# Four column strips of a modulation product in one tile, and the second layer's later ones moved into the dense feed-forward

## The chip, the cores and the metric

One core of a Trainium2 chip runs the kernel. The time is device microseconds from start to end of one launch. Three runs of the kernel before took 2573.72, 2575.47 and 2582.24 us; their median is 2575.47 us.

## What is computed

Two layers of a backbone work on 256 latent tokens behind 256 context tokens, with 1024 features each. A layer is a modulated norm, a token mixer of three parts (S5, gated DeltaNet, Mamba-2) and a residual, then a second modulated norm, a feed-forward and a residual. The first layer has a dense feed-forward, the second one a top-2-of-8 expert feed-forward. Cut to what matters here:

```python
for i in range(DEPTH):                                   # DEPTH = 2
    ml = jnp.split((sc @ ada_w[i] + ada_b[i])[:, None, :], 6, axis=-1)   # latent modulation
    mc = jnp.split(sx @ ada_w[i] + ada_b[i], 6, axis=-1)                 # context modulation
    h_lat = modulate(x_lat, norm1_g[i], ml[0], ml[1])
    h_ctx = modulate(x_ctx, norm1_g[i], mc[0], mc[1])
    y_ctx, y_lat = token_mixer(h_ctx, h_lat, w_in[i], s5_p, gdn_p, m2_p, not last)
    x_lat = x_lat + ml[2] * (y_lat @ w_out[i])
    x_lat = x_lat + ml[5] * ffn(modulate(x_lat, norm2_g[i], ml[3], ml[4]))
    # the same for x_ctx in the first layer
```

`ada_w[i]` has 1024 rows and 6144 columns, float32, 24 MB a layer. It meets only two vectors, `sc` and `sx`, so its product is a reading of 24 MB with little arithmetic.

## The kernel before

The work of the two layers is traced by one class, `Net`, and put in order by a scheduler. `band(b)` sets a priority: instructions traced in a lower band stand earlier, as far as their inputs and their buffers let them. All loads go through one queue, SP's, in that order, and each engine executes its instructions in that order. Pools of buffers are stacked on a left and a right side of the on-chip memory. A pool that is opened where another one lay waits for what used that place.

**The modulation product.** `ada` (L176) works out a third `g` of a layer's 6144 columns: 2048 columns, taken as four strips of 512. For each of the eight tiles `k` of 128 rows, and each strip, it loads a tile of `ada_w` (L184) and issues one matmul with the 32 columns of `sc` as the stationary operand (L157, through `mm`). The four strips use four different groups of 32 columns of the PE array (`tile_position`) and four groups of 32 partitions of one PSUM bank. The finished bank is copied to `adasb` (L190), transposed in four pieces (L193) and added to `mods` (L198). Third 0 of layer 0 is worked out in another function, `first_inputs`. Thirds 1 and 2 of both layers are traced in `mixer`, with tiles of one strip (`wd=512`, 256 KB, two buffers); third 0 of layer 1 is traced behind `mixer(0)` in the main function, with tiles of two strips (512 KB, four buffers). Third 1 holds the factor of the mixer's residual and the shift of the second norm, third 2 that norm's scale and the factor of the feed-forward's residual.

**The mixer.** `mixer` (L1206) projects the normed input, then runs three parts whose instructions are interleaved: gated DeltaNet (`gdn`, tiles `gd_` and `iv_`, a recurrence over chunks of 128 tokens), Mamba-2 (`m2`, tiles `m_`), and the read-out of S5 (`s5_out`, L621). `s5_out` takes four quarters in turn. A quarter loads `s5U`, `s5X`, eight pieces of `s5D` (L638) and two `s5V` (L643), all but `s5V` with one buffer, and issues 24 matmuls (48 records) on them. After each two quarters the result goes through a transpose, a skip and a gelu to memory (`geD`, L672). `s5_gate` (L677) then reads it back (`s5gL`, `s5gH`, L685), multiplies it with `s5_w_glu` and writes `yD` (L697). The other two parts write `yD` too (L1021 and L1189). At the end the pool `yo` is opened, on the same side as the S5 read-out and over its place; `yD` is read back and split in two parts (L1379, L1380), and `out_proj` (L1389) multiplies it with `w_out` and adds the residual (L1407).

Layer 0 has the pool `ad` of the modulation tiles on the left, below `s5_out`'s pool `s5o`; the right side has the pool of `gdn`, whose lowest tiles are `gd_ncs`, `gd_oss`, `gd_rs` and `iv_X`.

**Feed-forwards.** `ffn` (L1410) takes the 22 tiles of hidden features in four strips of 6, 5, 6 and 5: gate and up products, silu, and the down product added to the residual. `moe` (L1450) loads all experts' weights (`mwr`, L1651), whose first loads wait for residuals of the second mixer.

Of the kernel before, what the change touches and what calls it, by code (L numbers as in the profile page):

```python
# [10 lines left out]
F32 = mybir.dt.float32  # L11
# [4 lines left out]
PSUM = bass.MemoryType.PSUM  # L16
# [3 lines left out]
KT = 8  # L20
T = 512
# [10 lines left out]
# Places of the layers' parts in the schedule (bands relative to the layer's own), buffers and PSUM banks.  # L32
# [53 lines left out]
class Net:  # L86
# [41 lines left out]
    @contextmanager  # L128
    def band(self, b):
        """Instructions traced inside are scheduled behind those of lower bands."""  # L130
        tc, outer = self.tc, self.cur
        if b == outer:
            yield
            return
        self.cur, old = b, tc.cur_priority
        tc.cur_priority = self.bands.get(b, int(b * 100000))
        yield
        self.bands[b] = tc.cur_priority
        self.cur, tc.cur_priority = outer, old
# [9 lines left out]
    def psum_split(self, **banks):  # L149
        """The PSUM banks of each use from here on in the trace."""  # L150
        self.turn = {tag: cycle(ids) for tag, ids in banks.items()}
# [24 lines left out]
    def ada(self, l, g, p, tag, bufs, wd=1024):  # L176
        nc = self.nc
        W = self.A["ada_w"][l]
        ps = self.ps("ad")
        for k in range(KT):  # L180
            w = []
            for c0 in range(g * 2048, (g + 1) * 2048, wd):
                t = p.tile([128, wd], F32, name="ada", tag=tag, bufs=bufs)
                nc.sync.dma_start(t, W[k * 128:(k + 1) * 128, c0:c0 + wd])  # L184
                w += [t[:, i:i + 512] for i in range(0, wd, 512)]
            for j in range(4):
                self.mm(ps[32 * j:32 * j + 32, :], self.sc[:, k, :], w[j],
                        start=(k == 0), stop=(k == KT - 1), tile_position=(0, 32 * j))
        sb = p.tile([128, wd], F32, name="adasb", tag=tag, bufs=bufs)[:, :512]
# [10 lines left out]
    def mod_ab(self, l, which, ks=slice(0, KT)):  # L200
        """Per-feature factor and shift of one modulated norm, [128, 8, 2]; the factors of the tiles ks are worked out."""
# [10 lines left out]
    def first_inputs(self, p, pw, hH, hL):  # L212
        """Shift and scale of the first norm, two feature tiles at a time, their part of the normed input, and its products with
        the first columns of w_in as they come."""
# [41 lines left out]
    def rsqrt(self, pool, out, v, shape, s=1.0, e=EPS, eps_ap=None, bufs=1):  # L256
        nc = self.nc
        y0 = pool.tile(shape, F32, name="rs_y", tag="rs_y", bufs=bufs)
        h = pool.tile(shape, F32, name="rs_h", tag="rs_h", bufs=bufs)
        t = pool.tile(shape, F32, name="rs_t", tag="rs_t", bufs=bufs)  # L260
# [7 lines left out]
    def norm_stats(self, pool, x, early):  # L268
        """1 / rms of x: [128, 8, n], the same in all partitions; early: the band of the sums of squares."""
# [14 lines left out]
    def norm_tile(self, pool, x, r, ab, hH, hL, k, perm=False):  # L284
        """Feature tile k of the norm times a plus b; x: [128, 8, T]."""
# [20 lines left out]
    def wload(self, src, nk, ncol, keep=None):  # L306
        """src: [nk*128, ncol] in DRAM; the parts of each k tile, in the pool keep if there is one."""
# [18 lines left out]
    def mm3(self, ps, w, h, first, last, tiles=None):  # L326
        """ps += w^T h over the k tiles, w and h as (high, low) lists per tile."""
# [7 lines left out]
    def proj(self, l, c0, ncol, h, t0):  # L335
        """[ncol <= 128 columns of w_in]^T h -> PSUM [ncol, T - t0]."""
# [10 lines left out]
    def exp_acc(self, p, out, x, shape):  # L347
# [17 lines left out]
        # below the range of the reduction the result is zero  # L365
        nc.vector.scalar_tensor_tensor(out, x, -87.0, y, op0=OP.is_ge, op1=OP.mult)

# [1 line left out]
    def s5_tables(self, l, side, lo, hi, U=None, B=None, lam=None):  # L369
        """Per-layer tables of the S5 scan in chunks of 8 tokens, kept in DRAM; lo and hi are the bands of its Vector part and  # L370
        of the rest. With U, the first table is applied to it at once and the powers go to lam."""
# [8 lines left out]
        with tc.tile_pool(name="s5tab", bufs=1, side=side, reuse_waits="tile") as p, self.band(lo):  # L380
# [27 lines left out]
            # gamma = (lam_bar - 1) / lam  # L408
# [25 lines left out]
            # the powers 8, 16, ... 256 for the scan  # L434
# [15 lines left out]
            # the powers act on B, and their conjugates on conj(C)  # L450
# [15 lines left out]
            for q in range(4):  # L466
# [17 lines left out]
                with self.band(hi):  # L484
# [26 lines left out]
                    # k-th lag: rows (direction, input); lag 0 sums the directions  # L511
# [30 lines left out]
    def s5_inputs(self, p, j, u, U):  # L542
        """Channel tile j of the scan's input in chunks: U[(token in chunk, channel), group, chunk]."""
# [17 lines left out]
    def s5_own(self, G, U, B, g0):  # L561
        """The chunks' own states of four groups, to the places of the states that enter the next chunks."""
# [11 lines left out]
    def s5_states(self, l, U, B, side):  # L574
        """The chunks' own states by the table in DRAM."""
# [9 lines left out]
    def s5_scan(self, l, p, B, lam):  # L585
        """The states that enter the chunks, kept in DRAM: a scan by doubled strides, up and down."""
# [3 lines left out]
        def add(e, i0, n):  # L590
            """B[i] += lam^(8 * 2^e) B[i - 2^e], n places i0, i0 + 2 * 2^e, ..."""
# [29 lines left out]
    def s5_out(self, l, uD, UD, XD, yD, t0, side):  # L621
        """Scan outputs, skip, gelu and gate; the result goes to yD[0:4]."""
# [78 lines left out]
    def smalls(self, l, p, tp, h):  # L701
# [15 lines left out]
        # softplus = max(x, 0) + log1p(exp(-|x|)), log1p by 2 atanh(e / (2 + e))  # L717
# [15 lines left out]
        # both parts, four heads of each in turn  # L733
# [10 lines left out]
        # cs: decay from the chunk's start through each token; de: from each token to the end; tot  # L744
# [16 lines left out]
    def decay_quad(self, p, sm, t, h0, out, tag, bufs):  # L761
        """out[s, h, c] = decay between tokens s and c of chunk t (forward above the diagonal)."""
# [13 lines left out]
    def conv_silu(self, p, ps, w, b, out):  # L776
        """ps: [128, n] of whole 256-token segments; out: [128, n]."""
# [18 lines left out]
    def gdn_tok(self, p, tp, src, n, out, ss, t_first, h):  # L796
        """Token-major copy of one head's [128, n] tile to DRAM, and each token's sum of squares."""
# [32 lines left out]
    def gdn_prep(self, p, tp, kT, qT, bs, sm, t0):  # L830
        """Decayed key products of the chunks and the inverses of their 16 x 16 diagonal blocks."""
# [55 lines left out]
    def gdn(self, l, p, kT, qT, vD, kD, prep, nrm, bs, ks, qss, sm, szD, yD, t0, b0):  # L887
        """kT: [128, 4, 512]; qT: [128, 4, 512 - t0]; vD, kD: token-major [128, chunk, head, 128]; b0: the first band of
        the layer."""
# [21 lines left out]
        def inverses(gr):  # L911
            """(I + U)^-1 of strictly triangular matrices, by doubling the diagonal blocks; U[s] = beta[s] kw[s]."""
# [32 lines left out]
        def step(t, d, Y, last):  # L945
            """One chunk of the recurrence."""
# [52 lines left out]
        def outs(pair):  # L999
            """rmsnorm and gate; the query norm and its scale act only through eps"""  # L1000
# [51 lines left out]
    def m2_decays(self, p, sm, WD, first):  # L1052
        """WD[s, chunk, head, c]: the weight of token s's step in token c, before the product of their B and C."""
# [13 lines left out]
    def m2(self, l, p, g, sm, mD, WD, yD, t0):  # L1067
        """One group of 8 heads, a generator of three stages for each pair of chunks. mD: x (4 tiles), silu(z) (4), B, C, feature-major; the normed and gated result goes
        to yD."""
# [17 lines left out]
        def states(pair):  # L1087
            """The inputs of two chunks and the states entering them."""
# [81 lines left out]
        def gate(pair, ins):  # L1170
            """Gate and norm of the outputs of two chunks."""
# [11 lines left out]
            r = p.tile([128, 256], F32, name="m2_r", bufs=1)  # L1183
            self.rsqrt(p, r, pn[:, :256], [128, 256], 1.0 / 512)
# [21 lines left out]
    def mixer(self, l):  # L1206
# [35 lines left out]
        if l == 1:  # L1242
            pa, qa = self.pool("ad", sa)
# [24 lines left out]
        with self.band(b0 + q_["sc"]):  # L1268
            # as large as the input's pool at least, so the next pool keeps clear of it
            pt, qt = self.pool("s5t", sb)  # L1270
            XD = self.s5_scan(l, pt, B, lam)
# [57 lines left out]
        # the second gates, and the inputs of the state space part, one kind first or in turn  # L1329
# [14 lines left out]
        for g in (1, 2):  # L1344
            with self.band(b0 + q_[f"ab{g}"]):
                self.ada(l, g, pa, "ad", 2, 512)
        with self.band(b0 + q_["sb"]):
            self.s5_out(l, uD, UD, XD, yD, t0, sa)
        with self.band(b0 + q_["m2"]):
            p, q2 = self.pool("m2", sb)  # L1350
            # the first stage of a pair of chunks is traced before the last one of the pair before it
# [31 lines left out]
        qa.close()  # L1383
        if l == 0:
            qg.close()
            qm.close()
        self.dbg(f"x_mix{l}", self.xT)

    def out_proj(self, l, part, y, t0):  # L1389
        """The rows of w_out in the blocks part of 512."""  # L1390
# [7 lines left out]
    def residual(self, l, mod0, m, ps, t0, perm=False):  # L1398
        """x[m] += gate * ps"""
# [10 lines left out]
    def ffn(self, l, side):  # L1410
# [10 lines left out]
        for nj in (6, 5, 6, 5):  # L1421
# [22 lines left out]
            j0 += nj  # L1444
        q.close()
# [4 lines left out]
    def moe(self, l):  # L1450
# [13 lines left out]
        # units of the first weights, where later tokens and results go  # L1464
# [34 lines left out]
    def route(self, p, rw, ab, htp, Pm, gate, rk, iota, cnt):  # L1499
        """Top-2 routing and the dispatch of the tokens. The tokens are normed without the factors a and shifts b of their  # L1500
        features here; the logits take them by the router's rows, the experts' inputs after the dispatch."""
# [367 lines left out]
    def run(self):  # L1869
# [9 lines left out]
        with self.band(R["ff"]):  # L1879
            self.ffn(0, "right")  # L1880
# [72 lines left out]
```

## Time and profile before

| | before |
|---|---|
| runs | 2573.72, 2575.47, 2582.24 us |
| profiled execution: span, mean granted clock | 2572.8 us, 0.968 |
| PE busy | 2380.3 us, 93% |
| VectorE (DVE) busy | 1866.4 us, 73% |
| ScalarE (ACT) busy | 1441.9 us, 56% |
| GpSimd (POOL) busy | 375.1 us, 15% |
| moved by DMA | 543.87 MB, mean 211 GB/s |

The profile has no other time of its own execution than its span; the median of the runs is 2.7 us above that. Stages by the first and last instructions of their tiles: the first mixer runs to about 760 us, the dense feed-forward to about 1165, the second mixer to about 1735, the experts to the end. A line number of a matmul says little, since nearly all are recorded at L157; they are told apart by the tiles that they write and read (`bank<-ada,sc` is the modulation product). [...] "PEclk" and the clock column of a window are the granted TensorE clock as a share of full speed (2.4 GHz). DMA is the mean busy share of the 16 DMA engines.

### The profile page before, as it was taken

The page shows a single profiled execution, that of the slowest core. Times are in us where ns is not written, and L with a number is a line of the kernel's source. Part 1 is how long each engine was busy: PE and PEld are TensorE (multiplying, and loading weights), DVE is VectorE, ACT ScalarE, POOL GpSimd, SP SyncE. Part 2 cuts the span into 40 slices and gives each one's busy share as a digit, 9 for nine tenths or more (in the row PEclk, how much of TensorE's full clock was granted, in tenths as well). Part 3 has the DMA queues.
Part 4 walks back from the last instruction along what each step waited for, and adds up shares of the span by engine and source line. Part 5 has one row for each costly group of instructions (what it writes and reads, how often), then busy time and mean ns, then how long its engine had stood idle before and what let it go on. Part 6 is the DMA issues. An engine that isn't in the chain of part 4 may idle for free. (4 is left out here: it accounts for less than half of the span.)

```text
span 2572.8 us, 36182 instructions
## 1 busy us (share of the span) xinstructions
PE 2380.3 (93%) x12758; PEld 1862.0 (72%) x12758; DVE 1866.4 (73%) x3011; ACT 1441.9 (56%) x2223; POOL 375.1 (15%) x435
## 2 busy tenths in 40 slices
PE   7999876899999999998987799999999999999997
PEld 4778755656666888885875666587888888888876
DVE  8686998446548675445688954468888888888886
ACT  4676556433234554335766632347777777777765
POOL 0011677312000000000074621100000000000000
PEclk9899988999999999998999899999999999999999
DMA  7444422786634445333554466588999999999994
GB/s 245 117 122 116 122 91 74 238 248 213 231 114 159 144 132 175 103 87 106 163 139 118 152 195 185 172 258 294 346 340 345 347 343 344 348 344 345 349 344 148
DMA packets 474156, 543.87 MB, mean 211 GB/s; under 512 B 29040, under 2 KB 298864, under 8 KB 473712
## 3 DMA queue, kind: packets, MB, share of 16 engines
q1 hardware_dynamic: 473968, 541.50, 64.6%
q8 instruction: 102, 1.67, 0.3%
q14 instruction: 86, 0.70, 0.1%
HBM read 487.87 MB, written 53.54 MB: 210 GB/s over the span
## 5 line engine op out<-in xcount | busy, mean ns | idle before, releaser
L1661 DVE TENSOR_TENSOR mwL<-mwr,mwH 128x2048 fp32r<-128x2048 f32 (+1 forms) x272 | 605.0, 2226 | 95.7 <-PE bank L157 58.8
L1660 ACT ACTIVATE mwH<-mwr 128x2048 fp32r<-128x2048 f32 (+1 forms) x272 | 508.1, 1868 | 202.7 <-PE bank L157 166.5
L320 ACT ACTIVATE wH<-wr 128x512 fp32r<-128x512 f32 (+2 forms) x388 | 232.9, 605 | 395.2 <-PE bank L157 281.6
L321 DVE TENSOR_TENSOR wL<-wr,wH 128x512 fp32r<-128x512 f32 (+2 forms) x388 | 281.7, 729 | 221.7 <-ACT wH L320 200.8
L157 PE MATMUL bank<-mwL,xeH 128*128 128x512 f32 (+1 forms) x768 | 292.7, 381 | 9.3 <-DVE mwL L1661 9.3
L157 PE MATMUL bank<-mwH,xeL 128*128 128x512 f32 (+1 forms) x768 | 288.1, 375 | 0.0
L157 PE MATMUL bank<-mwH,xeH 128*128 128x512 f32 (+1 forms) x768 | 284.6, 376 | 1.7 <-ACT mwH L1660 1.7
L157 PE MATMUL bank<-hH,wL 128*128 128x512 f32 (+2 forms) x656 | 249.8, 381 | 20.1 <-DVE wL L321 20.0
L157 PE MATMUL bank<-hH,wH 128*128 128x512 f32 (+2 forms) x656 | 246.8, 384 | 19.6 <-ACT wH L320 7.4
L157 PE MATMUL bank<-hL,wH 128*128 128x512 f32 (+2 forms) x656 | 248.7, 379 | 1.1 <-DVE hL L298 1.1
L157 PE MATMUL bank<-ada,sc 128*32 128x512 f32 (+1 forms) x576 | 147.8, 495 | 26.6 <-DMA ada<-in_ada_w_dram 25.6
L157 PEld LDWEIGHTS bank<-mwL,xeH 128*128 128x128 f32 x768 | 144.3, 188 | 37.7 <-DVE mwL L1661 11.7
L792 DVE SCALAR_TENSOR_TENSOR cv_acc<-cv_raw,pp,cv_acc 128x512 f32<-128x512 f32 (+1 forms) x192 | 161.6, 854 | 12.1 <-issue 6.1
L157 PEld LDWEIGHTS bank<-mwH,xeH 128*128 128x128 f32 x768 | 144.1, 188 | 31.4 <-ACT mwH L1660 2.5
L157 PEld LDWEIGHTS bank<-mwH,xeL 128*128 128x128 f32 x768 | 144.3, 188 | 26.4 <-DVE xeL L1626 0.2
L157 PEld LDWEIGHTS bank<-hH,wL 128*128 128x128 f32 (+1 forms) x656 | 126.6, 193 | 48.0 <-DVE wL L321 25.3
L157 PEld LDWEIGHTS bank<-hH,wH 128*128 128x128 f32 (+1 forms) x656 | 126.2, 193 | 47.5 <-ACT hH L297 9.4
L157 PEld LDWEIGHTS bank<-hL,wH 128*128 128x128 f32 (+1 forms) x656 | 126.7, 193 | 25.9 <-DVE hL L298 2.9
L157 PE MATMUL bank<-mwL,eaH 128*128 128x512 f32 x352 | 139.2, 395 | 0.0
L157 PE MATMUL bank<-fhH,wH 128*128 128x512 f32 x352 | 136.9, 393 | 2.3 <-ACT fhH L297 1.4
L157 PE MATMUL bank<-fhL,wH 128*128 128x512 f32 x352 | 138.8, 394 | 0.0
L157 PE MATMUL bank<-mwH,eaL 128*128 128x512 f32 x352 | 138.6, 394 | 0.0
(440 smaller groups left out, 4714.4 us busy)
## 6 DMA issues: line engine op xcount, KB each, us to landing
mwr<-in_moe_w_gate_dram SPq DMA_DIRECT2D x88, 1024.0 KB, 5.8
mwr<-in_moe_w_up_dram SPq DMA_DIRECT2D x88, 1024.0 KB, 5.4
mwr<-in_moe_w_down_dram SPq DMA_DIRECT2D x80, 1024.0 KB, 5.6
ada<-in_ada_w_dram SPq DMA_DIRECT2D x160, 256.0 KB, 4.1
wr<-in_w_in_dram SPq DMA_DIRECT2D x160, 256.0 KB, 3.1
wr<-in_w_out_dram SPq DMA_DIRECT2D x64, 256.0 KB, 3.2
wr<-in_ffn_w_gate_dram SPq DMA_DIRECT2D x44, 256.0 KB, 2.9
wr<-in_ffn_w_up_dram SPq DMA_DIRECT2D x44, 256.0 KB, 2.9
```

The costliest lines, as they stand in the source:

```text
L157: return self.nc.tensor.matmul(*a, **k)
L320: nc.scalar.activation(wH, w, AF.Copy)
L321: nc.vector.tensor_tensor(wL, w, wH.bitcast(F32), op=OP.subtract)
L792: nc.vector.scalar_tensor_tensor(acc, raw[:, :, j:j + 256], w[:, j:j + 1], acc, op0=OP.mult, op1=OP.add)
L1660: nc.scalar.activation(wH, w, AF.Copy)
L1661: nc.vector.tensor_tensor(wL, w, wH.bitcast(F32), op=OP.subtract)
```

## The change

- `ada` loads one tile `[128, 4, cw]` that holds `cw` columns of all four strips of a row tile, in one DMA. Then it issues the four strips' matmuls. The columns are taken in turns of `cw`.
- Layer 0, thirds 1 and 2: `cw=256` with two buffers, 32 loads of 512 KB where 64 of 256 KB were. The pool takes 2 x 4 KB a partition, where it took 2 x 2 KB. Pool `s5o` above it begins 4 KB higher, and its last tile, the second `s5u`, now lies where `gd_ncs`, `gd_oss`, `gd_rs` and the first `iv_X` lay.
- Layer 1, third 0: `cw=512` with three buffers, 8 loads of 1 MB where 16 of 512 KB were. Thirds 1 and 2 leave `mixer(1)`, where they were 64 loads of 256 KB; they are traced in `ffn`, after its first and its second strip, with the same pool (16 loads of 1 MB). That pool stays open through the feed-forward.
- The PSUM banks are split anew ahead of the feed-forward.
- The gate of Mamba-2 works out its reciprocal root in the tile of its squares (`m2_sq`), and the pool of `m2` is 4 KB a partition smaller.

```diff
-    def ada(self, l, g, p, tag, bufs, wd=1024):
+    def ada(self, l, g, p, bufs, cw):
         nc = self.nc
-        W = self.A["ada_w"][l]
+        W = self.A["ada_w"][l][:, g * 2048:(g + 1) * 2048].rearrange("k (j c) -> k j c", j=4)
         ps = self.ps("ad")
-        for k in range(KT):
-            w = []
-            for c0 in range(g * 2048, (g + 1) * 2048, wd):
-                t = p.tile([128, wd], F32, name="ada", tag=tag, bufs=bufs)
-                nc.sync.dma_start(t, W[k * 128:(k + 1) * 128, c0:c0 + wd])
-                w += [t[:, i:i + 512] for i in range(0, wd, 512)]
-            for j in range(4):
-                self.mm(ps[32 * j:32 * j + 32, :], self.sc[:, k, :], w[j],
-                        start=(k == 0), stop=(k == KT - 1), tile_position=(0, 32 * j))
-        sb = p.tile([128, wd], F32, name="adasb", tag=tag, bufs=bufs)[:, :512]
+        for c0 in range(0, 512, cw):
+            for k in range(KT):
+                w = p.tile([128, 4, cw], F32, name="ada", tag="ada", bufs=bufs)
+                nc.sync.dma_start(w, W[k * 128:(k + 1) * 128, :, c0:c0 + cw])
+                for j in range(4):
+                    self.mm(ps[32 * j:32 * j + 32, c0:c0 + cw], self.sc[:, k, :], w[:, j], start=(k == 0), stop=(k == KT - 1),
+                            tile_position=(0, 32 * j), skip_group_check=True)
+        sb = p.tile([128, 4, cw], F32, name="adasb", tag="ada", bufs=bufs).rearrange("p j c -> p (j c)")[:, :512]
...
-            r = p.tile([128, 256], F32, name="m2_r", bufs=1)
-            self.rsqrt(p, r, pn[:, :256], [128, 256], 1.0 / 512)
+            r = sq[:, 0]
+            self.rsqrt(p, r, pn[:, :256], [128, 256], 1.0 / 512, tiles=[sq[:, i] for i in (1, 2, 3)])
...
-        if l == 1:
-            pa, qa = self.pool("ad", sa)
...
         if l == 0:
             pa, qa = self.pool("ad", sa)
-        for g in (1, 2):
-            with self.band(b0 + q_[f"ab{g}"]):
-                self.ada(l, g, pa, "ad", 2, 512)
+            for g in (1, 2):
+                with self.band(b0 + q_[f"ab{g}"]):
+                    self.ada(l, g, pa, 2, 256)
...
-    def ffn(self, l, side):
+    def ffn(self, l, side, between):
...
             j0 += nj
+            if between:
+                between.pop(0)()
...
-            self.ada(1, 0, p, "ada", 4)
+            self.ada(1, 0, p, 3, 512)
             self.s5_tables(1, "left", R["tl1"], R["th1"])
-            q.close()
         self.wband = R["ffw"]
+        self.psum_split(mm=(0, 1), px=(2, 3, 4), bg=(5, 6, 7), ad=(2, 3))
         with self.band(R["ff"]):
-            self.ffn(0, "right")
+            self.ffn(0, "right", [lambda g=g: self.ada(1, g, p, 3, 512) for g in (1, 2)])
+        q.close()
```

The change moves instructions at three places. On the PE's queue in layer 0, before the change, the first read-out matmuls of S5 (`s5D`, `s5V`) stand among the recurrence's (`gd_`), Mamba-2's (`m_`) and the modulation's (`ada`):

```order
L157 MATMUL bank_5759<-s5D,s5U 64x128
L157 MATMUL bank_6147<-m_E,m_xt 64x128 x3
L157 MATMUL bank_3755<-gd_S_3565,xT 128x128
L157 MATMUL bank_5525<-ada,sc 32x512
L157 MATMUL bank_3755<-gd_S_3565,xT 128x128 x3
L157 MATMUL bank_5525<-ada,sc 32x512
L157 MATMUL bank_6147<-cst,m_yo 128x128 x3
L157 MATMUL bank_3765<-gd_r,iv_X 128x128 x4
L157 MATMUL bank_5759<-s5V,s5X 64x128
```

With the change, the PE's queue has these same two tiles first behind the last step of the recurrence and the last product of Mamba-2's gate:

```order
L157 MATMUL bank_4188<-gd_vb,gd_A 128x128 x4
L157 MATMUL bank_6594<-m_sq,cst 128x256 x4
L157 MATMUL bank_7281<-ada,sc 32x512 x4
L1014 MATMUL bank_4223<-cst,gd_o 128x128
L1014 MATMUL bank_4232<-cst,gd_o 128x128
L157 MATMUL bank_7281<-ada,sc 32x512 x4
L1014 MATMUL bank_4223<-cst,gd_o 128x128 x3
L1014 MATMUL bank_4232<-cst,gd_o 128x128 x3
L157 MATMUL bank_7281<-ada,sc 32x512 x20
L157 MATMUL bank_5759<-s5D,s5U 64x128
L157 MATMUL bank_5759<-s5V,s5X 64x128 x2
```

All of the read-out's matmuls have moved behind the recurrence and Mamba-2, and seven of the eight row tiles of layer 1's third 0 stand ahead of them.

SP's queue with the change, at the end of layer 0's recurrence (`yD<-gd_y` is its last store; the 1 MB `ada` loads are layer 1's third 0, the `s5` loads the first quarter of the read-out):

```order
L185 DMA ada<-in_ada_w_dram 128x2048 x4
L1187 DMA yD_90<-m_z 128x4x256
L185 DMA ada<-in_ada_w_dram 128x2048
L1019 DMA yD_90<-gd_y 128x2x256 x2
L185 DMA ada<-in_ada_w_dram 128x2048 x2
L631 DMA s5U<-UD_586 128x512
L633 DMA s5X<-XD_1897 128x1024
L636 DMA s5D<-KD_814 16x8x128 x8
L641 DMA s5V<-VD_815 128x1024 x2
```

The first load of the read-out has moved behind the recurrence's last store; before, it stood ahead of loads of the recurrence itself (`gd_vp`, `gd_ktk`), and the quarters were spread among them.

In the feed-forward the PE's queue now holds layer 1's third 1 (`bank_9187`) and third 2 (`bank_9882`) among the products of the hidden features (`fhH`, `fhL`):

```order
L157 MATMUL bank_9187<-ada,sc 32x512 x12
L157 MATMUL bank_8345<-nm_a,cst 128x512
L157 MATMUL bank_9187<-ada,sc 32x512 x8
L157 MATMUL bank_8461<-fhH,wH 128x512
L157 MATMUL bank_8498<-fhH,wH 128x512
L157 MATMUL bank_8461<-fhL,wH 128x512
```

Five of the eight row tiles of third 1 stand around the norm, the last three between the first products; the four strips of third 2's row tiles do not all stay together (its 32 matmuls stand in rows of 4, 2, 1, 1, 1, 9, 1, 7, 1 and 5).

## Rows read from the trace of the kernel before

**Rows 1.** The page's second part: the span in 40 equal slices.

```profile
PE   7999876899999999998987799999999999999997
PEclk9899988999999999998999899999999999999999
```

**Rows 2.** Busy time by stretch, layer 0's mixer (columns as in the first line).

```profile
core 0: us, PE busy (x) PEld busy (x) DVE busy (x) ACT busy (x) POOL busy (x), PEclk, DMA share, GB/s
500.00:550.00 50.00, 46.66 (x309) 28.46 (x308) 24.27 (x51) 15.85 (x42) 12.63 (x12) 0.97 0.88 254
550.00:600.00 50.00, 50.00 (x306) 32.24 (x304) 26.86 (x54) 17.34 (x39) 7.54 (x7) 1.00 0.62 198
600.00:650.00 50.00, 48.05 (x263) 28.23 (x262) 28.79 (x61) 16.79 (x45) 12.93 (x12) 1.00 0.66 222
```

**Rows 3.** Groups of instructions, 460 to 700 us, tiles `ada`: PE.

```profile
L157 PE MATMUL bank<-ada,sc 128*32 128x512 f32 x116 | 52.3, 615 | 5.5 <-DMA ada<-in_ada_w_dram 5.4
```

**Rows 4.** PE's timeline: start, length, instruction; groups of modulation matmuls.

```profile
560.51 1.04 PE L157 MATMUL bank<-ada,sc 128*32 128x512 f32 x2
599.03 1.05 PE L157 MATMUL bank<-ada,sc 128*32 128x512 f32 x4
767.12 1.92 PE L157 MATMUL bank<-ada,sc 128*32 128x512 f32 x16 [0.86 <-PE bank L193]
```

**Rows 5.** Tile views, 460 to 640 us: duration in ns, first and last start in us.

```profile
L157 PE MATMUL bank<-s5D,s5U x64: 272/273/324, 491.0 to 570.1; 128*64 128x128 f32 x64
L638 SPq DMA_DIRECT2D s5D<-KD x32: 303/426/457, 474.8 to 557.1; - x32
L157 PE MATMUL bank<-s5V,s5X x128: 272/273/324, 496.5 to 571.2; 128*64 128x128 f32 x128
DMA to landing us min/median/max: 4.1/5.7/7.2
```

**Rows 6.** Tile views of layer 0's gelu, gate and read-back for `w_out`.

```profile
L685 ACT ACTIVATE s5gH<-s5gL x4: 622/631/645, 586.1 to 590.5; 128x512 fp32r<-128x512 f32 x4
L157 PE MATMUL bank<-s5gL,wH x16: 390/394/498, 591.6 to 615.9; 128*128 128x512 f32 x16
L697 SPq DMA_DIRECT2D yD<-s5yy x4: 327/330/339, 603.8 to 618.4; - x4
L1379 ACT ACTIVATE yo<-yr x8: 1041/1058/1062, 657.9 to 694.3; 128x1024 fp32r<-128x1024 f32 x8
```

**Rows 7.** Last stores of the recurrence and of Mamba-2, layer 0.

```profile
L1021 SPq DMA_DIRECT2D yD<-gd_y x4: 383/411/467, 536.5 to 647.4; - x4
L1189 SPq DMA_DIRECT2D yD<-m_z x2: 385/386/387, 651.1 to 680.3; - x2
```

**Rows 8.** Tile `yo` alone: its matmuls' ends and its busy time (columns as above, without POOL).

```profile
L157 PE MATMUL bank<-yo,wL x128: 392/399/502, 661.2 to 759.0; 128*128 128x512 f32 x128
650.00:760.00 110.00, 92.07 (x384) 71.46 (x384) 9.96 (x8) 8.43 (x8) 1.00 0.55 175
```

**Rows 9.** Busy time by stretch: the norm ahead of the feed-forward, the feed-forward.

```profile
760.00:800.00 40.00, 33.60 (x129) 13.64 (x128) 26.02 (x100) 16.34 (x32) 0.56 (x2) 0.96 0.62 204
800.00:850.00 50.00, 50.00 (x223) 40.45 (x222) 42.28 (x167) 22.40 (x35) 0.00 (x0) 1.00 0.42 122
```

**Rows 10.** Tile `ada` alone by stretch: PE, PEld, clock, DMA share, GB/s.

```profile
760.00:800.00 40.00, 16.15 (x66) 2.36 (x64) 0.96 0.62 204
1480.00:1600.00 120.00, 27.30 (x61) 3.69 (x62) 1.00 0.66 198
1600.00:1660.00 60.00, 20.00 (x41) 2.74 (x42) 1.00 0.53 164
1660.00:1740.00 80.00, 14.99 (x28) 1.82 (x26) 0.95 0.77 246
```

**Rows 11.** Busy time by stretch, layer 1's mixer.

```profile
1540.00:1600.00 60.00, 58.77 (x396) 38.87 (x396) 28.43 (x56) 12.77 (x32) 10.43 (x9) 1.00 0.66 198
1600.00:1660.00 60.00, 56.45 (x344) 37.12 (x344) 26.14 (x54) 19.04 (x52) 6.52 (x7) 1.00 0.53 164
```

**Rows 12.** Waits of SP's queue, 460 to 760 us: total, times, longest.

```profile
SPq L184 <- PE bank L157: 65.0, 45, 4.3
```

**Rows 13.** Busy time by stretch, where the PE has idle time.

```profile
400.00:450.00 50.00, 33.19 (x194) 28.22 (x194) 43.05 (x53) 31.60 (x68) 37.44 (x29) 0.79 0.19 69
```

More of the change, by code (lines that the diff above doesn't have):

```diff
@@ L253, in first_inputs, with rsqrt @@
         return pu
-    def rsqrt(self, pool, out, v, shape, s=1.0, e=EPS, eps_ap=None, bufs=1):
+    def rsqrt(self, pool, out, v, shape, s=1.0, e=EPS, tiles=None):
         nc = self.nc
-        y0 = pool.tile(shape, F32, name="rs_y", tag="rs_y", bufs=bufs)
-        h = pool.tile(shape, F32, name="rs_h", tag="rs_h", bufs=bufs)
-        t = pool.tile(shape, F32, name="rs_t", tag="rs_t", bufs=bufs)
+        y0, h, t = tiles or [pool.tile(shape, F32, name=f"rs_{x}", tag=f"rs_{x}", bufs=1) for x in "yht"]
         nc.vector.tensor_scalar(h, v, s, e, op0=OP.mult, op1=OP.add)
@@ L1382, in mixer @@
         q.close()
-        qa.close()
         if l == 0:
+            qa.close()
             qg.close()
```

## The prediction

> **What bounds the kernel now.** I read the page's slices first. The PE is at nine tenths or more in most of the span [rows 1], so a stage's time is mostly the PE's queue, and a matmul that goes away is time only where the PE is full. I went on to the three stages that the change touches. In layer 0's mixer the PE is busy 46.66, 50.00 and 48.05 us of three stretches of 50 [rows 2]: the recurrence, Mamba-2, the S5 read-out and the modulation fill each other's gaps. The modulation has 52.3 us of it from 460 to 700 us [rows 3]. In the feed-forward the PE has no idle time at all; in the norm ahead of it 6.4 us of 40 [rows 9]. In layer 1's mixer it is busy 58.77 of 60 us and 56.45 of 60 [rows 11], with 62.3 us of modulation in the three stretches of rows 10. Behind that the experts follow and shift with it.
>
> **What a group costs.** One strip's matmul (two records) takes 1.04 us, two strips together (four records) take 1.05, and eight matmuls, two row tiles of four strips, take 1.92 [rows 4]. So strips that stand together cost what one does: about 0.96 us for four. In the mixers they come one by one or in pairs, since each is a tile of its own with two buffers behind one queue. With four in one tile a group costs 0.96 us, one of half width 0.48 by the same row (estimate).
>
> **Layer 0, what it removes.** 32 groups of half width, 15.4 us, replace 52.3: 37 us less on a PE that is full. The waits of SP's queue for that ring, 65.0 us [rows 12], shrink in count (32 loads for 64), but the buffers are still two; I count nothing for that. It is covered by the PE having work, and if that cover is gone, a late load is a wait on the PE's queue.
>
> **Layer 0, what it moves.** The order shows the whole S5 read-out behind the recurrence and Mamba-2. Its pool starts 4 KB higher and its last tile lies on the recurrence's first ones, so it waits for them. Before, its four quarters ran from 474.8 to 571.2 us and its gate ended at 618.7 [rows 5, 6], hidden between the other parts. Now nothing is left to stand between. The new chain, step by step:
> - The other parts end, before at 647.4 and 680.3 us [rows 7]. Without some 30 us of S5 matmuls and 37 of modulation ahead of them they end earlier, at best at 580 for the recurrence; the recurrence is serial, though, and I take 610, near the middle of 580 and 647.
> - Layer 1's third 0 stands ahead on both queues, seven loads of 1 MB with three buffers: 10 us (four loads at the 254 GB/s of rows 2 are 16; some run earlier).
> - Four quarters, one after the other, since all tiles but `s5V` have one buffer. A quarter has 12 issues, eight of them at 0.43 us, so some 5 us, then 5.7 us to the last landing [rows 5], then 24 matmuls, whose 48 records of 0.273 us overlap, some 5 us with the copy: 15.5, and 62 for four. The least would be 10 each (issues beside the matmuls before), 40.
> - From the last matmul (571.2) to the read-back of the gelu (586.1 [rows 5, 6]) 15 us.
> - The gate: 586.1 to 618.7 before, with other work between; 48 matmuls and two vector steps alone are some 16.
> - Store, read-back and split for `w_out`: a landing of some 4 us twice and 1.06 us [rows 6] with its second half, 11.
>
> That is 610+10+62+15+16+11 = 724, where `yo` began at 657.9. `out_proj` has 92.07 us of its own on the PE [rows 8], some 8 less than the 101 that it took beside leftovers; with its start, 94. It ends at 818 instead of 760: **+58**. Bounds: 580 and 40 for the quarters, no wait for third 0, give 756, so -4; 647 and a gate of 32 give 871, so +111. The middle is nearest to the rows, since each step there has its own duration.
>
> **The norm and the feed-forward.** Third 0 of layer 1, 16.15 us [rows 10], leaves the norm. Five groups of third 1 take its place, 4.8 us. The PE had gaps there, so I count a gain of 7 of these 11. Then three groups of third 1 and some 14 of third 2 (it stands in pieces of 4, 2, 1, 1, 1, 9, 1, 7, 1, 5) come on a full PE: 17 x 0.96 = 16.3, and eight transposes 1.3. Nothing covers these: **+10**, between 0 (all in fours, all 11 gained) and 18 (nothing gained).
>
> The Trainium skill, "TensorEngine Tiling (Array Packing)", section "Tiling Modes", says that a change of tiling mode drains the PE. By that, each scattered piece in the feed-forward would cost two drains beside its matmuls; the page gives no price. The trace shows no sign of one that can be told from the 1.04 us of a group standing alone against 0.96 in a row [rows 4], so at most 0.08 for each.
>
> **Layer 1's mixer.** 62.3 us of modulation leave it [rows 10]. 27.30 us of them lie where the PE is full, and I count 70% as time, 19; 20.00 lie in the recurrence's end, where they stood partly in its gaps (the PE is idle 3.55 us in spite of them [rows 11]), 45%, 9; 14.99 lie beside `out_proj`, 75%, 11. That is **-39**. Bounds: -62 if all was time, -20 if the serial recurrence sets most of it. The 16 MB that are no longer loaded there free SP too, counted within. What is late next is the recurrence itself.
>
> **Sum.** +58 +10 -39 = +29. The profiled span is 2572.8 us, so 2601.8; the median of the runs is 2.7 above that span, so 2604.5, say **2605**. The other edits (reciprocal root in another tile, banks) add no instructions; at nothing they rest on the same vector steps, and on POOL and ACT with idle time in every stretch.
>
> **Rivals.**
> *Faster.* The PE's saved time is what counts, and the S5 chain is nearly hidden. For it: the PE is the full engine in both mixers. Against: the order. If the other parts end at 580 and a quarter takes 10 us (its queue is free then), `yo` starts at 580+40+15+16+11 = 662 and ends at about 756: -4. With +10 and -39 it is -33, so 2542. It decides from the point at which `out_proj` ends less than 29 us later than before. Chance 0.17 for all of this side (some of it by -62 in layer 1).
> *No change.* `out_proj` ends 21 to 37 us late, and layer 1 pays it back: about 2575. Chance 0.13.
> *Slower still.* In the exposed chain the PE is idle for most of 110 us. Where it was busy 33.19 of 50 us, the granted clock was 0.79 [rows 13]; at the lower level, 1.2 GHz, the matmuls of quarters and gate take twice as long, some 10 us more, and the start of `out_proj` some 5; with the recurrence ending at 630 it is +35: 2640. The Trainium skill, "TensorE: Matmul & The Clock Gate", Part 1, has an idle PE fall to half its clock and a busy one rise again; rows 13 agree in kind. Chance 0.15, within slower.
> *The strips don't stay together.* If each of the 32 matmuls of third 2 ran alone, they would cost 32 x 1.04 = 33 us rather than 13: 2625. Rows 4 speak against it, the order in part for it. Chance 0.07, within slower.
>
> **Chances.** The forecast itself (a net loss of some 8 to 50 us) has 0.48; with the two other slow cases 0.70 for slower by over 0.3%, 7.7 us, about what a measurement of this kernel can tell from no change. Same 0.13, faster 0.17. The range is 2560 to 2645: below it lies most of the faster case, above it the far end of the slow ones, together 2 in 10. The slow cases alone, in their own 8 of 10, span 2586 to 2650.
>
> **What would show it.** Right: the profile after has a stretch of some 100 us around 620 to 720 with the PE half idle and the clock below 1, in which the releasers of PE's waits are `s5D`, `s5V` and `s5gL`; the first `yo` split stands near 724 and layer 0's last residual near 818; layer 1's mixer is some 39 us shorter from the end of the feed-forward to the first expert; `ada` groups in fours take 0.96 us. Wrong: the `s5D` matmuls overlap the recurrence after all, or the first `yo` split stands before 690, or layer 1 is shorter by 60.

## The result, and the profile after

The changed kernel takes 2611.45 us (median of 4 runs, 2607.12 to 2613.59) against 2574.59 for the kernel before in the same comparison (4 runs, 2573.57 to 2582.24). The ratio is 1.0135 (95% interval 1.012 to 1.015): slower by 37 us, where 2605 (+29) was forecast. The profiled execution, the fastest of the four, has a span of 2605.3 us, 32.5 more than before; the stages below account for these 32.5.

The page's slices after the change, to be laid beside [rows 1]:

```profile
PE   7999875896489999999897779888999999999997
PEclk9899987998789999999999989988999999999998
```

Slices 10 to 12 have fallen, with a 4 and a clock of 7; that is the end of layer 0's mixer. Busy time there by stretch (PE, PEld, DVE, ACT, POOL, clock, DMA share, GB/s), to be laid beside [rows 2]:

```profile
550.00:600.00 50.00, 48.59 (x394) 37.38 (x393) 37.72 (x81) 12.00 (x36) 9.58 (x9) 1.00 0.46 150
600.00:650.00 50.00, 29.54 (x198) 16.16 (x196) 12.82 (x33) 7.29 (x25) 9.14 (x8) 0.80 0.89 313
650.00:700.00 50.00, 19.56 (x160) 16.07 (x160) 4.44 (x8) 4.44 (x7) 0.00 (x0) 0.69 0.67 210
700.00:760.00 60.00, 45.10 (x162) 34.66 (x163) 26.93 (x38) 23.20 (x32) 0.00 (x0) 0.83 0.61 184
```

Where the PE was full it now does 19.56 us of work in 50, at a granted clock between its two levels. What it waits for, the first five rows of the PE's waits between 600 and 760 us:

```profile
PE bank L157 <- DMA s5D<-KD: 25.9, 4, 8.9
PE bank L157 <- DMA ada<-in_ada_w_dram: 10.5, 7, 4.3
PE bank L157 <- ACT yo L1375: 7.9, 1, 7.9
PE bank L157 <- DMA s5V<-VD: 7.1, 8, 1.6
PE bank L157 <- ACT s5gH L683: 6.7, 1, 6.7
```

Four waits for `s5D`, one a quarter, then the gelu's way back (`s5gH`) and the read-back for `w_out` (`yo`): the chain of the forecast, link by link. The tile views give its dates (duration in ns, first and last start in us), beside [rows 5 to 8]:

```profile
L1019 SPq DMA_DIRECT2D yD<-gd_y x4: 384/568/842, 535.0 to 621.3; - x4
...
L636 SPq DMA_DIRECT2D s5D<-KD x32: 302/424/547, 624.5 to 685.9; - x32
L157 PE MATMUL bank<-s5D,s5U x64: 272/421/477, 638.4 to 695.8; 128*64 128x128 f32 x64
L157 PE MATMUL bank<-s5V,s5X x128: 272/421/476, 640.0 to 696.3; 128*64 128x128 f32 x128
L683 ACT ACTIVATE s5gH<-s5gL x4: 629/630/631, 704.4 to 708.0; 128x512 fp32r<-128x512 f32 x4
L695 SPq DMA_DIRECT2D yD<-s5yy x4: 319/326/455, 715.6 to 724.1; - x4
L1375 ACT ACTIVATE yo<-yr x8: 1056/1060/1062, 729.1 to 749.5; 128x1024 fp32r<-128x1024 f32 x8
L157 PE MATMUL bank<-yo,wL x128: 389/392/629, 732.1 to 823.3; 128*128 128x512 f32 x128
```

No quarter starts before the recurrence's last store at 621.3 us. Stage by stage (us): layer 0's mixer ends with the last start of a `yo` matmul, the feed-forward and layer 1's mixer each with the last start of a residual (`xT`), the experts with the span:

| | layer 0's mixer ends | feed-forward | layer 1's mixer | experts | span |
|---|---|---|---|---|---|
| before | 759.0 | 404.5 | 569.7 | 839.6 | 2572.8 |
| after | 823.3 | 411.9 | 529.1 | 841.0 | 2605.3 |
| difference | +64.3 | +7.4 | -40.6 | +1.4 | +32.5 |
| forecast | +58 | +10 | -39 | 0 | +29 |

The first column is a time from the start, the next three are lengths. Layer 0's last start is the row above and [rows 8]; the feed-forward's and layer 1's last residuals start at 1235.2 and 1764.3 us (1163.5 and 1733.2 before):

```profile
L1403 DVE SCALAR_TENSOR_TENSOR xT<-bank,mods,xT x66: 469/476/486, 823.8 to 1235.2; 128x256 f32<-128x256 f32 x66
...
L1403 DVE SCALAR_TENSOR_TENSOR xT<-bank,mods,xT x32: 476/479/485, 1701.0 to 1764.3; 128x256 f32<-128x256 f32 x32
```

### The profile page after: what moved, and what is told of

Its sections match the earlier page's. It is cut to its first block, busy times and chain, and to the rows that moved or that the text cites. A ratio compares the mean times of both kernels' runs of the same rounds, so it can differ in the third digit from the quotient of the medians.

```text
span 2605.3 us, 36301 instructions
## 1 busy us (share of the span) xinstructions
PE 2331.0 (89%) x12886; PEld 1878.7 (72%) x12886; DVE 1867.5 (72%) x3011; ACT 1437.8 (55%) x2220; POOL 373.8 (14%) x435
## 5 line engine op out<-in xcount | busy, mean ns | idle before, releaser
L157 PE MATMUL bank<-yo,wH 128*128 128x512 f32 (+1 forms) x512 | 134.8, 356 | 15.8 <-ACT yo L1375 12.0
```

What stands on the lines that cost most here:

```text
L157: return self.nc.tensor.matmul(*a, **k)
```

## The experiments

Theory A, that of the forecast: 4 KB more in a pool move the S5 read-out behind the recurrence, and that alone costs layer 0 its time; the rest of the change gains. Theory B: the four-strip tiles themselves, large loads with two buffers, hold up layer 0. Twelve kernels ran. The stages of all of them, in the same columns as above, with the median of the runs. The stages are those of the one profiled execution, which can stand off the median by some us (e4's is 7 us below it, e6's and e10's are 6 above). Layer 1's mixer took between 529.1 and 534.6 us in the six kernels that have the change's layer 1, so a few us there say nothing.

| run | layer 0's mixer ends | feed-forward | layer 1's mixer | experts | median |
|---|---|---|---|---|---|
| e1, before with 4 KB more | 838.1 | 393.6 | 568.2 | 840.2 | 2642.62 |
| e2, four inverse buffers | 752.6 | 409.1 | 533.4 | 840.2 | 2536.10 |
| e3, quarter strips, two buffers | 749.3 | 427.2 | 534.6 | 841.2 | 2553.54 |
| e4, layer 0 as before | 762.8 | 423.8 | 530.3 | 840.5 | 2566.18 |
| e5, thirds in layer 1, half strips | 751.9 | 393.7 | 618.1 | 858.1 | 2623.37 |
| e6, the same, quarter strips | 755.5 | 393.5 | 561.8 | 841.5 | 2548.55 |
| e7, before, loads without matmuls | 758.1 | 404.8 | 544.4 | 840.5 | 2548.42 |
| e8, before with four inverse buffers | 774.6 | 399.0 | 570.6 | 839.9 | 2584.99 |
| e9, shared ring in the read-out | 748.2 | 409.4 | 534.2 | 840.8 | 2534.79 |
| e10, quarter strips, three buffers | 770.4 | 410.5 | 534.4 | 841.1 | 2552.38 |
| e11, e6 without matmuls | 758.5 | 391.8 | 548.8 | 838.7 | 2537.42 |
| e12, e7 with short loads | 761.1 | 404.6 | 544.2 | 842.1 | 2549.80 |

**The place alone (e1).**

```diff
+            pad = pa.tile([128, 1024], F32, name="adpad", bufs=1)
+            nc.vector.memset(pad[:, 0:1], 0.0)
```

> The kernel before, with 4 KB a partition of unused place added to layer 0's pool of modulation tiles and nothing else: the S5 read-out then stands behind the recurrence, as with the change, while the strips stay single. Theory A (the place of the pool costs layer 0 its time): slower by 60 to 100 us, about 2660, since the chain of quarters, gelu and gate stands alone and the single strips (52 us) still stand ahead of it; the first yo split near 750 us instead of 658. Theory B (the loads of 512 KB and the half groups cost layer 0 its time, the place does not): within 10 us of before, 2575 to 2585.

Measured: 2642.62 us, ratio 1.026 (1.0243 to 1.0277). Unused memory made the kernel slower by 67 us, layer 0's mixer by 79. Its read-out, in the same view as above:

```profile
L157 PE MATMUL bank<-s5D,s5U x64: 272/421/476, 650.9 to 710.5; 128*64 128x128 f32 x64
```

The strips are single here, so theory B has nothing to work with. Theory A holds: the place is enough. It costs more than in the change (79 against 64), and the first read-out matmul comes 12.5 us later (650.9 against 638.4), with single strips still running there until 661 us. The feed-forward takes 11 us less; layer 1's third 0 now runs beside the chain instead of in the norm.

**The place taken away (e2).**

```diff
-    ... iv=5 ...
+    ... iv=4 ...
```

> The changed kernel, with four instead of five buffers for the inverses (iv_X) in layer 0, which takes 2 KB from the recurrence's pool, so that the S5 read-out's pool lies clear of it. Theory A: the read-out stands among the recurrence again and layer 0 loses its 64 us, so 2574.6 - 39 (layer 1) + 7 (feed-forward) = 2543, and less by up to 25 for the strips that now run four together: 2520 to 2545. Theory B: layer 0 stays late by 40 us or more, above 2590. A third way: four buffers slow the inverses by some us, the gain of the strips is eaten, 2545 to 2555.

Measured: 2536.10 us, ratio 0.9842 (0.9826 to 0.9859). The tiles are those of the change, and B, above 2590, is refuted. All of layer 0's loss is gone, and it ends 6 us ahead of before. The read-out stands among the recurrence again:

```profile
L157 PE MATMUL bank<-s5D,s5U x64: 272/273/324, 496.4 to 566.0; 128*64 128x128 f32 x64
```

**Two other ways round it (e3, e4).** e3 has `cw=128` in layer 0; e4 keeps the old one-strip `ada` for layer 0's thirds 1 and 2.

```diff
-                    self.ada(l, g, pa, 2, 256)
+                    self.ada(l, g, pa, 2, 128)                 # e3
+                    self.ada1(l, g, pa, "ad", 2, 512)          # e4, ada1 is the function before
```

> The changed kernel, with a quarter of a strip's width in a tile in layer 0 (cw=128, two buffers, 64 loads of 256 KB), so that the pool takes 4 KB as before. Theory A: as in the run with four inverse buffers, 2520 to 2550; the pieces of 512 bytes in a load may cost it some 5 to 10 us against that run. Theory B (four strips in one tile with two buffers starve the PE): above 2575.

> The changed kernel, with layer 0's thirds 1 and 2 as before the change (tiles of one strip, 64 loads, two buffers of 2 KB). What is left of the change is layer 1's part. Theory A: 2574.6 - 39 + 7 - some us for third 0 in fours = 2540 to 2548. What it stands above the two runs before it is what four strips together are worth in layer 0: up to 25 us if the PE is the bound there, under 5 if the recurrence's own chain is.

Measured: 2553.54 us (0.9915, 0.9898 to 0.9931) and 2566.18 us (0.9962, 0.9949 to 0.9974). e3 has four strips in a tile and refutes B again; e4, with single strips in layer 0, ends it later than e2 and e3, which B would not have. Both missed their ranges: e3 by a few us above its range, e4 by 18. The table says where: not in layer 0 (749.3 and 762.8, where e4's single strips cost 13 us over e3, as A allows), but in the feed-forward, 427.2 and 423.8 against 409.1. In both, layer 0's third 2 ends behind `out_proj`, layer 1's third 0 runs in the norm, and thirds 1 and 2 both behind it. So the stage in which a third runs has a price: without any third the norm and the feed-forward take 393.5 (e6), with third 0 in pairs of strips 404.5 (before), with two thirds in fours 409.1 (e2), with three 427.2 (e3). That is 8 us for each of the first two in fours, 11 for the one in pairs and 18 for the last.

**The same in layer 1 (e5, e6).** On e2, layer 1's thirds 1 and 2 go back into its mixer, in tiles of four half strips (e5, 8 KB) or four quarter strips (e6, 4 KB).

```diff
-            self.ffn(0, "right", [lambda g=g: self.ada(1, g, p, 3, 512) for g in (1, 2)])
+            self.ffn(0, "right", [])
...
+                    self.ada(l, g, pa, 2, 256)                      # e5
+                    self.ada(l, g, pa, 2, 256 if l == 0 else 128)   # e6
```

> The changed kernel with four inverse buffers in layer 0 (so that layer 0's read-out lies clear), and layer 1's thirds 1 and 2 back in its mixer, with tiles of four half strips (8 KB a partition in layer 1's pool of modulation tiles). In the order, layer 1's S5 read-out now stands behind its recurrence. Theory A (the place of a pool decides): layer 1's mixer pays what layer 0's did, a chain of some 62 + 15 + 12 + 11 us behind the recurrence less what ends earlier, 45 to 75 us more than the next run: 2565 to 2610. Rival: the read-out is on nobody's path in layer 1, within 15 us of the next run.

> As the run before, but with tiles of four quarter strips in layer 1 (4 KB, as before the change), so that its read-out stands among the recurrence as before the change. If layer 1's gain came from the PE time of single strips (62 us, here 64 groups of 0.24 us = 15), layer 1 keeps 25 to 30 of its 36 us without the move, and the norm and feed-forward get back 10 to 19 us: 2520 to 2540. If the gain came from the loads leaving (16 MB, 128 issues on SP's queue), layer 1 is back at some 570 us and the total is 2555 to 2570.

Measured: 2623.37 us (1.0182, 1.0161 to 1.0204) and 2548.55 us (0.9892, 0.987 to 0.9914). The wider tiles with their 4 KB cost 75 us in layer 1, at the top of the 45 to 75 expected and above the total's range: 56 in the mixer, 17 in the experts. The experts' first 36 us ran at a granted clock of 0.53 with the PE busy 21.62 us, in e6 at 0.86 with 28.32; the rest of their loss is open. In e5 the recurrence's last store and the read-out stand apart:

```profile
L1019 SPq DMA_DIRECT2D yD<-gd_y x2: 359/362/366, 1540.3 to 1540.9; - x2
...
L157 PE MATMUL bank<-s5D,s5U x64: 272/323/476, 1599.5 to 1671.7; 128*64 128x128 f32 x64
```

It is not the same picture as in layer 0, though. The whole order has turned round: in e6 the recurrence ends last (its last store at 1652.1 us, the read-out's last `s5D` matmul at 1602.4); in e5 it ends first, at 1540.9, and the modulation (first load at 1575.8 instead of 1474.5) and the read-out come behind it, beside Mamba-2 (last store at 1628.4 instead of 1578.4). The PE also waits 30.5 us for `ada` loads between 1500 and 1720 us (19.7 in e6, 1450 to 1700), which is what theory B would look like. e5 differs from e6 in the tiles' width as well as in the place, and no run added the place alone in layer 1; there the place as the cause is argued, not shown.

e6 is a miss of mine. Strips in fours take 33.09 us of the PE there instead of 62.29 (the tile `ada` alone, 1430 to 1740 us), where 15 were expected, because a group of four quarter strips standing alone takes 0.42 us and not a quarter of 0.96:

```profile
1478.22 0.42 PE L157 MATMUL bank<-ada,sc 128*32 128x128 f32 x8
```

Layer 1's mixer kept only 8 of the 40 us. So more than the PE's time left with the change; the next three runs price the two parts.

**What left layer 1 (e7, e11, e12).** e7 is the kernel before with all loads and, of layer 1's thirds 1 and 2, the last row tile's matmuls alone (it leaves out the other seven eighths of that product); e11 is the same on e6; e12 is e7 with loads of 32 columns for those row tiles.

```diff
+            if l == 1 and g > 0 and k < KT - 1:
+                continue
...
+                cw = 32 if l == 1 and g > 0 and k < KT - 1 else wd       # e12
+                nc.sync.dma_start(t[:, :cw], W[k * 128:(k + 1) * 128, c0:c0 + cw])
```

> The kernel before, with layer 1's thirds 1 and 2 loaded as before in its mixer, but only the last of the eight row tiles multiplied (seven eighths of that product are left out). If it is the PE time, layer 1's mixer is shorter by 30 to 40 us: 2536 to 2546. If it is the loads on SP's queue and the DMA, it is shorter by under 10: 2565 to 2575.

> As the run e6 (layer 1's thirds in its mixer in quarter strips, four inverse buffers in layer 0), but of layer 1's thirds only the last row tile's matmuls are left; seven eighths of that product are left out, all loads stay. e6 kept 8 of 40 us in layer 1's mixer although its strips take 31 us of the PE less. If it is the loads of 512-byte pieces, layer 1's mixer stays above 555 us here. If it is the 31 us of matmuls that are left, it falls to the 544 of the run e7 or below.

> As the run e7 (before, layer 1's thirds loaded in its mixer, only the last row tile multiplied), but the loads whose row tile is not multiplied bring 32 columns instead of 512; their number, their place in the program and their ring of two stay. With e7 layer 1's mixer took 544 us, without any of these loads (the change) 529. If the 15 us are the bytes, it falls to some 530. If they are SP's queue, which waits at the ring for a landing before the recurrence's loads can go on, it stays at 540 to 546.

Measured: 2548.42 us (0.9895, 0.9862 to 0.9928), 2537.42 us (0.9839, 0.9823 to 0.9854) and 2549.80 us (0.9894, 0.9873 to 0.9915). Layer 1's mixer takes 569.7 us with loads and single strips, 561.8 with strips in fours, 544.4 and 548.8 with the loads and an eighth of the matmuls, 529.1 with neither. So 25 us of the gain go with seven eighths of the matmuls (55 us of the PE, 62.29 less 7.32), and 10 to 15 with what e7 still had (against 529.1 to 534.6 without it). e7's total missed its range by 2 us. For e6, which stands 28 us above e2's 533.4, the matmuls that e11 leaves out explain 13 (29 us of the PE, 33.09 less 4.00, so 45% again); the other 15 stay with what is left in e11, mostly loads. e11's 548.8 lies between its two readings, above 555 and 544 or below. The bytes are not the cause: seven of eight loads bring a sixteenth in e12, and its mixer takes 544.2. SP's queue in e7 and in e12, 1430 to 1660 us (total, times, longest):

```profile
SPq L184 <- DMA ada<-in_ada_w_dram: 26.1, 26, 3.6
```

```profile
SPq L185 <- DMA ada<-in_ada_w_dram: 12.7, 19, 1.9
```

Short loads halved this wait and changed the mixer by nothing. What is left is the number and the place of the issues on SP's queue, the eighth of the matmuls with its transposes (7.32 us of the PE, some 3 at the rate of the others), and the order that the scheduler makes around them. These weren't separated.

**A control, and the best of them (e8, e9, e10).** e8 is the kernel before with `iv=4`. e9 is the change with `s5U` and `s5u` in one ring, which takes 2 KB from the read-out's pool. e10 has three buffers of quarter strips, 6 KB.

```diff
-                U = p.tile([128, 8, 64], F32, name="s5U", bufs=1)
+                U = p.tile([128, 8, 64], F32, name="s5U", tag="s5u", bufs=2)     # e9
...
+                    self.ada(l, g, pa, 3, 128)                                   # e10
```

> The kernel before with four inverse buffers in layer 0, nothing else: a control for the run e2. Theory A: the fifth buffer is worth nothing, 2572 to 2582. Rival: fewer buffers change the order for the better by themselves, and part of e2's gain is theirs: under 2568.

> The changed kernel, with the read-out's s5U and s5u tiles in one ring of two buffers, so that its pool is 2 KB smaller and ends where the recurrence's begins; five inverse buffers, half-width tiles as in the change. Theory A: no overlap, layer 0 without the 15 us that four inverse buffers cost in the control, so 2520 to 2536, at or below the run e2. Rival: the fifth buffer is worth nothing once the strips run in fours, 2533 to 2540.

> The changed kernel, with three buffers of four quarter strips in layer 0 (6 KB, which ends the read-out's pool just where the recurrence's begins). Against the run e3 (two such buffers, 2553): if e3's loss came from layer 0's third 2 ending late and pushing third 0 into the norm and both later thirds into the full feed-forward (427 us there), three buffers bring it to some 409 us, 2530 to 2540. If it came from the short pieces of its loads, it stays at 2548 to 2556.

Measured: 2584.99 us (1.0036, 1.0023 to 1.0049, 3 us above its range), 2534.79 us (0.9825, 0.9808 to 0.9842) and 2552.38 us (0.9897, 0.9881 to 0.9913). Four inverse buffers gain nothing by themselves; they cost layer 0 16 us while the strips are single. So e2's gain is not theirs. With strips in fours the fifth buffer is worth 4 us of layer 0 at most (748.2 in e9 against 752.6), and the totals can't be told apart (e9's 2534.79 lies in both of its ranges). e9 is the change with its fault taken out, and it beats both kernels: 43 us under the kernel before in the same comparison (2577.85). Its output product and last residual, to be laid beside those of after:

```profile
L1375 ACT ACTIVATE yo<-yr x8: 1037/1057/1062, 638.5 to 684.8; 128x1024 fp32r<-128x1024 f32 x8
...
L1403 DVE SCALAR_TENSOR_TENSOR xT<-bank,mods,xT x32: 472/477/485, 1629.2 to 1691.8; 128x256 f32<-128x256 f32 x32
```

e10 did what was expected in the feed-forward (410.5 instead of e3's 427.2) and gave it back in layer 0 (770.4 instead of 749.3), where Mamba-2's last store comes at 715.4 us, 51 us later than in e3:

```profile
L1187 SPq DMA_DIRECT2D yD<-m_z x4: 367/370/599, 547.8 to 715.4; - x4
```

Its total lies in the range given to the other reading, short pieces, but by this other way. Why the scheduler put Mamba-2's last gate there wasn't tried.

## Why the prediction was right

**Layer 0, +58 forecast, +64 measured.** The mechanism is shown by both ends: the place added to the kernel before brings the loss (e1), the place taken from the change removes it (e2, e9). Its terms: the other parts ended at 621 instead of 610; the wait for third 0 was 3 us, not 10 (621.3 to the first `s5D` load at 624.5); the four quarters took 72 (624.5 to 696.3), not 62; the way back of the gelu 8 (to 704.4), not 15, where SP's queue holds nothing else; the gate 20, not 16; store, read-back and split 6 (724.1 to the first `w_out` product at 730.2), not 11. Three terms were too small by 25 us together and three too large by 19, which leaves the 6 that were missed. Under the first term lies a price that was too low: a group of four half strips took 0.64 us, not 0.48, so the 32 of them took 20.26 us of the PE instead of 15.4; how much of the 11 us that is, no run shows. The quarters can be taken apart by the PE's timeline and one stretch:

```profile
475.88 0.64 PE L157 MATMUL bank<-ada,sc 128*32 128x256 f32 x8
...
624.50:638.40 13.90, 5.59 (x25) 0.66 (x26) 0.00 (x0) 0.00 (x0) 0.00 (x0) 0.62 1.00 328
...
638.37 0.66 PE L157 MATMUL bank<-s5D,s5U 128*64 128x128 f32 x2 [3.56 <-DMA s5D<-KD]
...
645.09 0.68 PE L157 MATMUL bank<-s5V,s5X 128*64 128x128 f32 x5
...
654.64 0.66 PE L157 MATMUL bank<-s5D,s5U 128*64 128x128 f32 x2 [5.14 <-DMA s5D<-KD]
```

Their loads took what was forecast: 13.9 us to the first matmul, at a DMA share of 1.00 with third 0's loads in flight (part of the wait for third 0 is hidden here), then 8.9, 10.7 and 8.3 between quarters, 42 in all. The matmuls took 7.0 to 8.1 us a quarter, 30 in all, where 5 each were put. In them the PE waits 7.1 us for `s5V`, and much of the rest runs at a lower clock: a median of 421 ns at granted clocks of 0.80 and 0.69, where it was 273 [rows 5]. An estimate from the timeline (records 0.11 us apart at 0.42 us each, 0.055 at 0.27) makes the clock's part some 8 us; no run tried it by itself. The forecast had that as the rival "slower still", with 10 us for the matmuls of quarters and gate, and kept it out of its own sum; it belonged in it. The rival's other half, a slow start of `out_proj`, did not come: 93 us, as forecast.

The Trainium skill, "TensorE: Matmul & The Clock Gate", Part 1, has an idle PE fall to half its clock; the trace agrees in kind, with a granted clock of 0.69 where the PE was busy 19.56 of 50 us.

**Norm and feed-forward, +10 forecast, +7.4 measured.** Third 2 in its pieces takes 13.9 us of the PE (1.07 at 852 us, 12.87 between 860 and 960), where 14 groups at 0.96 were put at 13.4; the three late groups of third 1 stood alone:

```profile
839.20 1.06 PE L157 MATMUL bank<-ada,sc 128*32 128x512 f32 x8
842.69 1.07 PE L157 MATMUL bank<-ada,sc 128*32 128x512 f32 x8
845.73 1.07 PE L157 MATMUL bank<-ada,sc 128*32 128x512 f32 x8
```

Each of these matmuls leaves two records, so eight records in 1.06 us are four strips at once. The rival that they don't stay together had 33 us for third 2; it took 13.9. No sign of a cost for changing between whole and split array stands in them beyond the 0.1 us over 0.96.

**Layer 1, -39 forecast, -40.6 measured, by the wrong shares.** The step put the whole gain on the PE's time: 62.3 us at 45 to 75%, "the 16 MB that are no longer loaded there free SP too, counted within". The matmuls that e7 leaves out gave 25 us for 55, which is 45% all over, 28 us for 62.3; the rest, 10 to 15, went with the loads and what hangs on them. The size was right by luck, two errors that cancel.

**The rival "faster"** was priced from the same rows and set on how much of the chain stays hidden. It would have needed `out_proj` to end less than 29 us late; it ended 64 late. Its picture, both mixers profiting, is e9's, and there it is true: 43 us faster, where the rival had 33.

## What to carry to other kernels

In layer 0 the tiles that grew by 4 KB cost nothing by themselves (e2, e9). What a pool pushes onto another pool's old place can cost a whole stage its overlap (e1); look at the built order, where work that was spread among others suddenly stands in one block, and at what that block then waits for. When an engine is full, the time that a removed matmul gives back is a share (here 45%, in e7 and in e11), and work moved out of a full stage has a price where it lands, here 8 to 18 us for each third.

## What the runs showed of the hardware

Loads of 32 columns instead of 512 (a sixteenth of the bytes) left layer 1's mixer at 544.2 us against 544.4: the bytes of these loads did not count there. Four column strips standing alone among other matmuls took 1.06 us at 512 columns, 0.64 at 256 and 0.42 at 128, so a group of half or quarter width cost more than half or a quarter. In the exposed chain the granted clock was 0.69 over 50 us, although the PE still had 160 matmul records there; the read-out's took 421 ns in the median, where they took 273 at 0.97 to 1.00 [rows 2, 5].
